# Norm weight carried by the weights, sums of x kept in memory, and slots bound to operands in the two gate passes, with the mLSTM core's first tiles on those slots

## The chip, the core and the metric

The kernel runs on one core of one Trainium2 chip. A core has five engines, each with its own in-order queue: TensorE (PE, matmuls; its weight loads are shown as PEld), VectorE (DVE), ScalarE (ACT), GpSimd (POOL) and SyncE (SP), which here issues the transfers (DMAs). Instructions wait for each other through semaphores, so an instruction that waits holds up everything behind it in its own queue. The metric is device microseconds of one execution; lower is better.

## The reference

Two layers on 2048 + 256 tokens of width 1024: windowed attention, then a bidirectional mLSTM, each behind a norm and with a gated output. The change lies in the mLSTM layer and in what leads to it. What is computed there, cut to the essentials:

```
x2 = x + attention(rms_norm(x, g0))
xn = rms_norm(x2, g1)                      # x2 * rstd * g1
q, k, v, gates, o, z = split(xn @ w_in)    # 512, 512, 1024, 16, 1024, 1024 columns
h  = mlstm(q, k, v, gates)                 # forward and backward, chunks with carried state C, n, m
h  = rms_norm(h per head) * sigmoid(o) * silu(z)
y  = rms_norm(x2 + h @ w_out, final_g)
```

## The kernel before

**Tiles.** The tokens are 18 tiles of 128 (2048 tokens are 16 tiles, the 256 others two). Everything is float32; each operand of a product is split into a high part in the format that TensorE multiplies (ACT makes it: `hi`) and the rest (DVE makes it: `lo = x - hi`), and a product is three matmuls, hi*hi, hi*lo and lo*hi.

**Passes.** A projection of 1024 columns goes through `winograd_pass` (L335). It works on nine pairs of tiles. `quarters` (L200) loads the weight in sixteen pieces of 128 x 512 and splits them into weight slots. The first pair is multiplied in the plain way (L320 to L322); halfway through it `combinations` (L212) makes four combined operands t1 to t4 of the weight in place of loaded pieces, and the other eight pairs are multiplied by Winograd's form of Strassen's scheme, seven products instead of eight (L271 to L273). For it `winograd_x` (L237) makes four sums of the input pieces (L249, L250, L256, L261 on DVE) and splits seven operands for each pair. Five such passes run: z of the attention, its output, q and k of the mLSTM (`mlstm_qkv`, L639), and two for the gates o and z (`mlstm_gates_states`, L813; pass 0 and pass 1, together "the oz passes"), which also carry the backward state of the mLSTM, tile by tile. The narrower v and gate projections (L666 to L682) run in the plain way between the q,k pass and the oz passes.

**Norm.** `attn_out` (L603) adds the residual, takes the norm and transposes; the transposed tile leaves PSUM through a DVE multiplication by g1 (L633) and is stored as `xn2T`, the input of the q,k, v and oz projections.

**Gates.** `gate_sums` (L685) turns the gate columns of all tiles into running maxima and decay factors. It is one serial chain of small operations over PE, DVE and ACT: sums (L710, L716), a transpose (L723), a maximum (L725), a row of running maxima of 36 + 32 tiny DVE operations (L741, L744), exponentials (L748, L755), two scans (L767) and their exponentials (L768, L775). It is written ahead of the oz passes and its pool is called `gt`.

**Core.** `mlstm_core` (L864) runs over the tiles: weights of a tile (`E`, `El`, `Eh`, split v), four heads of numerators (L926, L928), the state update (L806), the gating (L944), and then the output projection of the tile before (`back`, L376 to L378 with the weight w_mo from L992), with the final norm.

**Order.** The code is recorded through a tile framework which then orders the instructions of each engine by a simulated timeline, so instructions of the next stage can stand among those of the stage before. Three things limit this: each queue runs in order; a tile whose memory was used before waits for the last reader of what lay there (the pools of different stages share addresses); SP issues transfers in eight lanes, and a transfer waits for the one eight before it. Weight slots are taken from one list, `self.free`, whichever is free first (L132). The sixteen slots of pool `wp` stay; eight more (`y0` to `y7` in pool `wy`, L1008) lie where the core's right-hand pool `b3y` (L869) comes to lie afterwards. The oz passes hold their gate tiles `e` and `s` in pool `b2`, which is opened before `b2s`, the pool of the backward state (L816, L817).

Of the kernel before, what the change touches and what calls it, by code (L numbers as in the profile page):

```python
# [48 lines left out]
KX, WL = 0, 0  # L49
# [12 lines left out]
class Trunk:  # L62
    def __init__(self, nc, tc, ctx, a):
# [120 lines left out]
    def part(self, raw, g=None):  # L184

        nc = self.nc
        hi, lo = self.slot()
# [12 lines left out]
    def quarters(self, src, c0, g=None):  # L200

        W = {k: [None] * 4 for k in ("b12", *WOPS)}
        for row in range(2):
            gk = lambda i: None if g is None else g[:, row * 4 + i:row * 4 + i + 1]
            for i in range(4):
                for col in range(2):
                    op = f"b{row + 1}{col + 1}"
                    W[op][i] = self.part(self.quarter(src, c0, row, col, i), gk(i))
# [3 lines left out]
    def combinations(self, src, c0, W, g=None):  # L212
# [9 lines left out]
        for i in range(4):  # L222
# [10 lines left out]
            for op, raw in (("t2", t2), ("t3", b12), ("t1", b11), ("t4", b21)):  # L233
                W[op][i] = self.part(raw)
                self.at[op, i] = self.taken.pop()

    def winograd_x(self, s0, s1, X):  # L237

# [4 lines left out]

        a11 = load(s0, 0)
# [5 lines left out]
        nc.vector.tensor_sub(x2, x1, a11)  # L250
        X["s2"] = self.split(x2)
# [4 lines left out]
        nc.vector.tensor_sub(a21, a11, a21)  # L256
        X["s3"] = self.split(a21)
# [3 lines left out]
        nc.vector.tensor_sub(a12, a12, x2)  # L261
# [73 lines left out]
    def winograd_pass(self, xT, src, c0, g, use, done=None, following=None, first=None):  # L335
# [267 lines left out]
    def attn_out(self, first):  # L603
        nc, tc, a = self.nc, self.tc, self.a
        with ExitStack() as st:
# [18 lines left out]
            def norm(t, x):  # L624
                rs = p.tile([128, 1], F32, tag="rs", name="rs", bufs=2)
                self.rms(p, x, rs[:])
                for b in range(2):
# [5 lines left out]
                    nc.vector.tensor_mul(xo[:], tp[:], self.g[:, 1, b * 4:(b + 1) * 4].unsqueeze(2).to_broadcast([128, 4, 128]))  # L633
# [155 lines left out]
    def weighted_k(self, p, t, d, raw=()):  # L789
# [4 lines left out]
        hi = p.tile([128, MH, DQK], F32R, tag="kh", name="kh", bufs=1)  # L794
        nc.gpsimd.tensor_mul(k, k, self.w[:, d, t, :].unsqueeze(2).to_broadcast([128, MH, DQK]))
# [17 lines left out]
    def mlstm_gates_states(self):  # L813
        nc, tc, a = self.nc, self.tc, self.a
        with ExitStack() as st:
            pe = st.enter_context(tc.tile_pool(name="b2", bufs=2, reuse_waits="tile"))  # L816
            p = st.enter_context(tc.tile_pool(name="b2s", bufs=1, reuse_waits="tile"))  # L817
# [22 lines left out]
            for b in range(2):  # L840
# [3 lines left out]
                def use(t, h, o, u, b=b):  # L844
# [5 lines left out]
                    nc.scalar.activation(e, o, AF.Sigmoid)  # L850
                    if h == 0:
                        (nc.vector if u is None else nc.gpsimd).tensor_mul(e, e, o)
                    if t not in part:
# [6 lines left out]
                X = self.winograd_pass(self.xn2T, a["w_oz"], b * 1024, None, use, lambda n, pair: back_state(NT - 1 - b * len(PAIRS) - n),  # L860
                                       self.xn2T[:2] if b == 0 else None, X)


    def mlstm_core(self, y):  # L864
        nc, tc, a = self.nc, self.tc, self.a
        with ExitStack() as st:
            pool = lambda n, **k: st.enter_context(tc.tile_pool(name=n, bufs=2, reuse_waits="tile", **k))
            TRP, TRT = self.sps, "s"
            py, pm, pv, p, pe = pool("b3y", side="right"), pool("b3m"), pool("b3v"), pool("b3"), self.early  # L869
            ps = pool("b3ps", space=PSUM)  # L870
            cm = py.tile([128, 2, 128], F32, tag="cm", name="cm", bufs=1)
# [7 lines left out]
            def weights(t):  # L879
# [8 lines left out]
                v = self.parts(pv, self.v[t], "v", 2)  # L888
                qs = (py if t % 2 else pv).tile([128, 2, MH, 128], F32, tag="qs", name="qs", bufs=1)
# [221 lines left out]
```

## Time and profile before

| | |
|---|---|
| time, median of 3 runs | 2311.11 us (2309.26 to 2311.87) |
| profiled execution | 2308.62 us |
| span of its profile | 2306.6 us |
| PE busy | 2216.3 us, 96% |
| DVE busy | 1561.6 us, 68% |
| ACT busy | 1094.6 us, 47% |
| POOL busy | 468.2 us, 20% |
| DMA | 326.41 MB |
| TensorE clock granted, mean | 0.987 |

The stages follow each other as: attention to about 700 us, its z gate and its output to 1094 us, q and k from there to 1300 us, v to 1490 us, the two oz passes to 1894.5 us, the core to the end. A row of the timeline reads: start, duration, engine, line, operation, out<-in with the tiles' names, shapes, count, and in brackets the idle time of the engine before it and what released it.

### The profile page before, as it was taken

The numbers are of one execution on the slowest core, as the hardware profiler recorded it, in microseconds if no ns is written. First come the engines' busy times: TensorE is split into PE (matmuls) and PEld (weight loads), VectorE is DVE, ScalarE is ACT, GpSimd is POOL, SyncE is SP. The second block draws the span as 40 slices with busy tenths as digits, with TensorE's granted clock in tenths as the row PEclk, the third lists the DMA queues.
The fourth block names the chain that finished last, engine by engine and source line by source line (L and its number), as shares of the span: only waits on it lengthen the run. The fifth ranks groups of instructions, "written<-read, shape, count | busy, mean of one in ns | idle before, by whom it ended". The sixth has DMA issues, their size and how long they took to land.

```text
span 2306.6 us, 32951 instructions
## 1 busy us (share of the span) xinstructions
PE 2216.3 (96%) x11102; PEld 1763.1 (76%) x11102; DVE 1561.6 (68%) x3403; ACT 1094.6 (47%) x2503; POOL 468.2 (20%) x392
## 2 busy tenths in 40 slices
PE   8999999999899999999899999999999987999998
PEld 7767676767567888788788899978877876888887
DVE  7565656565877779778656422487888676777784
ACT  6454545454764335445434311346454355455453
POOL 3211121211001222232000000022232234333320
PEclk9999999999999999999999999999999997999999
DMA  7111111111226447667534622344465456665642
GB/s 266 48 39 49 38 49 39 49 38 40 92 65 196 152 159 239 219 214 237 172 123 145 222 92 92 122 157 154 164 215 174 146 188 222 216 197 196 209 157 69
DMA packets 170281, 326.41 MB, mean 142 GB/s; under 512 B 18784, under 2 KB 21632, under 8 KB 170112
## 3 DMA queue, kind: packets, MB, share of 16 engines
q1 hardware_dynamic: 169968, 324.30, 42.2%
q8 instruction: 88, 1.44, 0.3%
q14 instruction: 81, 0.66, 0.1%
q10 hardware_dynamic: 144, 0.01, 0.0%
HBM read 235.34 MB, written 88.89 MB: 141 GB/s over the span
## 4 chain that ended last, share of the span: by engine, by line
PE 75%; DVE 10%; DMA 5%; ACT 4%; issue 3%; POOL 2%; SPq 0%; DVEq 0%; POOLq 0%; ACTq 0%
PE pj L376 9%; PE pj L378 9%; PE pj L377 9%; PE pj L271 4%; PE pj L272 4%; PE pj L273 4%; PE ptp L527 3%; PE o L539 3%; PE d L271 3%; PE d L272 3%; PE c L273 3%; PE d L273 3%; PE c L272 3%; PE c L271 3%; DMA qs<-rows 2%
## 5 line engine op out<-in xcount | busy, mean ns | idle before, releaser
L376 PE MATMUL pj<-whi,xhi 128*128 128x512 f32 (+2 forms) x1152 | 433.8, 378 | 8.6 <-ACT whi L167 5.6
L122 ACT CAST xhi<-rawx 128x512 fp32r<-128x512 f32 x372 | 228.3, 618 | 439.9 <-PE pj L377 106.4
L378 PE MATMUL pj<-whi,xlo 128*128 128x512 f32 (+2 forms) x1152 | 422.8, 372 | 5.2 <-DVE xlo L123 4.4
L377 PE MATMUL pj<-wlo,xhi 128*128 128x512 f32 (+2 forms) x1152 | 426.4, 370 | 0.0
L123 DVE TENSOR_TENSOR xlo<-rawx,xhi 128x512 fp32r<-128x512 f32 x338 | 246.0, 732 | 81.3 <-ACT xhi L122 73.5
L376 PEld LDWEIGHTS pj<-whi,xhi 128*128 128x128 f32 x1152 | 218.1, 189 | 50.8 <-issue 8.8
L378 PEld LDWEIGHTS pj<-whi,xlo 128*128 128x128 f32 x1152 | 217.7, 189 | 49.5 <-DVE xlo L123 8.6
L377 PEld LDWEIGHTS pj<-wlo,xhi 128*128 128x128 f32 x1152 | 217.9, 189 | 37.0 <-issue 2.4
L514 ACT ACTIVATE Sm<-Sm,nm 128x384 f32<-128x384 f32 (+1 forms) x288 | 167.1, 582 | 94.3 <-DVE nm L508 87.9
L271 PE MATMUL pj<-whi,xhi 128*128 128x512 f32 x480 | 193.9, 404 | 7.2 <-DVE u L286 2.7
L272 PE MATMUL pj<-wlo,xhi 128*128 128x512 f32 x480 | 192.3, 401 | 2.9 <-DVE wlo L190 2.9
L273 PE MATMUL pj<-whi,xlo 128*128 128x512 f32 x480 | 191.6, 400 | 0.0
L503 DVE CUSTOM_DVE_ANT_0 Sm<-s,mask 128x384 f32<-128x384 f32 (+1 forms) x272 | 136.0, 530 | 72.8 <-PE s L501 69.9
L527 PE MATMUL ptp<-ident,Sm 128*128 128x128 f32 x800 | 135.5, 280 | 10.0 <-DVE PT L530 6.6
L527 PEld LDWEIGHTS ptp<-ident,Sm 128*128 128x128 f32 x800 | 94.6, 141 | 54.6 <-ACT Sm L514 19.2
L271 PE MATMUL d<-whi,xhi 128*128 128x512 f32 x320 | 128.0, 400 | 0.0
L273 PE MATMUL c<-whi,xlo 128*128 128x512 f32 x320 | 127.3, 398 | 0.0
L272 PE MATMUL c<-wlo,xhi 128*128 128x512 f32 x320 | 127.3, 398 | 0.0
L271 PE MATMUL c<-whi,xhi 128*128 128x512 f32 x320 | 127.2, 397 | 0.0
L272 PE MATMUL d<-wlo,xhi 128*128 128x512 f32 x320 | 126.7, 396 | 0.0
L273 PE MATMUL d<-whi,xlo 128*128 128x512 f32 x320 | 126.6, 396 | 0.0
L500 PE MATMUL s<-KH,Q 128*128 128x384 f32 (+1 forms) x288 | 106.1, 380 | 10.3 <-DVE mx L503 4.6
(243 smaller groups left out, 4670.8 us busy)
## 6 DMA issues: line engine op xcount, KB each, us to landing
rawx<-xn2T SPq DMA_DIRECT2D x144, 256.0 KB, 3.1
x<-x SPq DMA_DIRECT2D x108, 256.0 KB, 3.9
rawx<-xT SPq DMA_DIRECT2D x72, 256.0 KB, 2.9
raww<-w_oz SPq DMA_DIRECT2D x64, 256.0 KB, 5.1
raww<-w_qkvg SPq DMA_DIRECT2D x40, 256.0 KB, 3.8
v<-v SPq DMA_DIRECT2D x18, 516.0 KB, 3.7
rawx<-v SPq DMA_DIRECT2D x36, 258.0 KB, 2.8
rawx<-x SPq DMA_DIRECT2D x36, 256.0 KB, 3.0
```

The lines of the kernel that those rows point to most:

```text
L122: nc.scalar.copy(hi[:], src)
L123: (eng or nc.vector).tensor_sub(lo[:], src, hi[:].bitcast(F32))
L271: nc.tensor.matmul(o, xh, wh, start=i == 0 and not more, stop=False, skip_group_check=more)
L272: nc.tensor.matmul(o, xh, wl, start=False, stop=False, skip_group_check=more)
L273: nc.tensor.matmul(o, xl, wh, start=False, stop=i == 3, skip_group_check=more)
L376: nc.tensor.matmul(o[:, :n], xh, wh, start=kt == 0, stop=False)
L377: nc.tensor.matmul(o[:, :n], xh, wl, start=False, stop=False)
L378: nc.tensor.matmul(o[:, :n], xl, wh, start=False, stop=kt == KT - 1)
L500: nc.tensor.matmul(S[:, :nk, :], q, KH[:, g, win, :], start=True, stop=False)
L503: nc.vector.tensor_tensor_reduce(Sm[:, :nk], S[:, :nk], mask[:, t % 3, win, :], 1.0, MASKED, ALU.add, ALU.max, mx[:, c:c + 1])
L514: nc.scalar.activation(Sg[c][:, :nk], Sg[c][:, :nk], AF.Exp, bias=nm[:, c:c + 1], scale=HD ** -0.5, accum_out=rs[:, c:c + 1])
L527: nc.tensor.transpose(tp[:, c, :], Ss[g][c][:, j, :], self.ident[:])
```

## The change

1. **Norm weight.** `attn_out` copies the transposed tile with ACT, without g1. The q,k pass, the v projection and the oz passes multiply g1 into their weights: the split of a piece becomes an ACT copy with a scale and a DVE operation with a scale, and `combinations` gets two ACT multiplications for each of its four steps.
2. **Sums of x.** The q,k pass stores the four sums of each of its eight Winograd pairs (32 stores of 256 KB). The oz passes load seven pieces per pair instead of four and make no sums.
3. **Slots.** In the oz passes an operand may have slots of its own: y0 to y3 hold only b11, y4 to y7 hold only b21 (pass 0) or t2 (pass 1). The v stage gets a list of slots without five of the free ones.
4. **Core.** The right-hand pool `b3y` holds what the core's first tiles need (v, qs, El, Eh of tile 0), other tiles alternate between pools; `cm` moves to the pool that is opened early; w_mo is loaded after six steps of the core's first tile, its transfers and splits ordered behind the last sigmoid of the oz passes; the weighted k of the forward state is made by four ACT copies with a scale and four DVE operations per tile instead of one POOL, one ACT and one DVE operation.
5. **Pools.** `b2s` is opened before `b2`.

```diff
-    def slot(self):
-        pool, tag = self.free.popleft()
+    def slot(self, op=None):
+        own = self.own.get(op)
+        others = [x for tags in self.own.values() for x in tags]
+        pick = next(x for x in self.free if (x in own if own else x not in others))
+        self.free.remove(pick)
+        pool, tag = pick
...
-    def winograd_x(self, s0, s1, X):
+    def winograd_x(self, s0, s1, X, sums=None):
+        if sums:
+            at = {"a11": (s0, 0), "a12": (s0, 1), "a22": (s1, 1), **{f"s{i + 1}": (s, 0) for i, s in enumerate(sums)}}
+            for op in XOPS:
+                X[op] = self.split(load(*at[op]))
+                yield
+            return
+        def keep(i, x):
+            if sums is not None:
+                d = self.dp.tile([128, 512], F32, tag=f"xs{len(self.xs)}_{i}", name="xsum")
+                made[i] = d
+                nc.sync.dma_start(d[:], x)
...
-                    nc.vector.tensor_mul(xo[:], tp[:], self.g[:, 1, b * 4:(b + 1) * 4].unsqueeze(2).to_broadcast([128, 4, 128]))
+                    nc.scalar.copy(xo[:], tp[:])
...
-            self.winograd_pass(self.xn2T, a["w_qkvg"], 0, None, use, first=first)
-            w = self.load_w(a["w_qkvg"][:, 1024:], [[512], [272, 256]])
+            self.winograd_pass(self.xn2T, a["w_qkvg"], 0, self.g[:, 1], use, first=first, sums=True)
+            kept = self.first + [[x for x in self.free if x not in self.first][-1]]
+            self.free = deque(x for x in self.free if x not in kept)
+            w = self.load_w(a["w_qkvg"][:, 1024:], [[512], [272, 256]], self.g[:, 1])
             self.release()
+            self.free.extendleft(reversed(kept))
...
+        if d == 0:
+            for h in range(MH):
+                wk = self.w[:, d, t, h:h + 1]
+                nc.scalar.activation(hi[:, h], k[:, h], AF.Copy, scale=wk)
+                nc.vector.scalar_tensor_tensor(lo[:, h], k[:, h], wk, hi[:, h].bitcast(F32), ALU.mult, ALU.subtract)
+            return hi, lo
...
+            p = st.enter_context(tc.tile_pool(name="b2s", bufs=1, reuse_waits="tile"))
             pe = st.enter_context(tc.tile_pool(name="b2", bufs=2, reuse_waits="tile"))
-            p = st.enter_context(tc.tile_pool(name="b2s", bufs=1, reuse_waits="tile"))
...
-                    nc.scalar.activation(e, o, AF.Sigmoid)
+                    self.gated = nc.scalar.activation(e, o, AF.Sigmoid)
...
-                X = self.winograd_pass(self.xn2T, a["w_oz"], b * 1024, None, use, lambda n, pair: back_state(NT - 1 - b * len(PAIRS) - n),
+                self.own = {"b11": self.first, "t2" if b else "b21": self.second}
+                X = self.winograd_pass(self.xn2T, a["w_oz"], b * 1024, self.g[:, 1], use, lambda n, pair: back_state(NT - 1 - b * len(PAIRS) - n),
...
-            py, pm, pv, p, pe = pool("b3y", side="right"), pool("b3m"), pool("b3v"), pool("b3"), self.early
+            py, pv, pm, p, pe = pool("b3y", side="right"), pool("b3v"), pool("b3m"), pool("b3"), self.early
...
-                v = self.parts(pv, self.v[t], "v", 2)
-                qs = (py if t % 2 else pv).tile([128, 2, MH, 128], F32, tag="qs", name="qs", bufs=1)
+                v = self.parts(pv if t % 2 else py, self.v[t], "v", 1)
+                qs = (pv if t % 2 else py).tile([128, 2, MH, 128], F32, tag="qs", name="qs", bufs=1)
...
-                El = p.tile([128, 2, MH, 128], F32R, tag="El", name="El", bufs=2)
+                El = (p if t % 2 else py).tile([128, 2, MH, 128], F32R, tag="El", name="El", bufs=1)
...
-            if not WL:
-                w += self.load_w(a["w_mo"], [[512]] * 2, self.g[:, 2], PH3, PL3)
...
-                    if t == 0 and i == WL and WL:
-                        w += self.load_w(a["w_mo"], [[512]] * 2, self.g[:, 2], PH3, PL3)
+                    if t == 0 and i == WL:
+                        with tc.issue_after(self.gated.ins):
+                            w += self.load_w(a["w_mo"], [[512]] * 2, self.g[:, 2], PH3, PL3)
```

**PE at the start of oz pass 0.** In the names, `um` is the maximum of `gate_sums`, `rw` its row of running maxima, `pl` and `pr` its PSUM tiles, `cu` the backward state's; `pj`, `c` and `d` are the PSUM tiles of the passes. Before, two excerpts where products of the chain stand:

```order
L271 MATMUL pj<-whi,xhi 128x512
L272 MATMUL pj<-wlo,xhi 128x512
L273 MATMUL pj<-whi,xlo 128x512
L272 MATMUL pj<-wlo,xhi 128x512
L728 MATMUL pr<-ident,um 1x72 x2
L273 MATMUL pj<-whi,xlo 128x512
L271 MATMUL pj<-whi,xhi 128x512
```

```order
L271 MATMUL pj<-whi,xhi 128x512
L753 MATMUL pl_14942<-rw,ones 128x144
L272 MATMUL pj<-wlo,xhi 128x512
L273 MATMUL pj<-whi,xlo 128x512
L750 MATMUL pl<-spr,ones 128x144
L271 MATMUL pj<-whi,xhi 128x512
```

After, the end of the plain pair (L347 to L349 are its matmuls now, L298 to L300 those of a Winograd pair):

```order
L349 MATMUL c<-whi,xlo 128x512
L936 MATMUL s<-qT,kT 128x128 x4
L759 MATMUL pr<-ident,um 1x72 x2
L784 MATMUL pl_15014<-rw,ones 128x144
L781 MATMUL pl<-spr,ones 128x144
L791 MATMUL pm<-ones,rw 72x1 x2
L804 MATMUL pM<-ident,MT 128x72 x2
L843 MATMUL cu<-vh,kh 128x258
L843 MATMUL cu<-v,kh 128x258
L843 MATMUL cu<-vh,kl 128x258
```

Nine matmuls into `cu` stand there, and behind them the first `L298` into `pj`. The chain's products stood one by one among the Winograd pairs (L728 in pair 1, L753 further on); now all of them stand in one row between the plain pair and the first Winograd pair.

**ACT at the same place.** `e<-pj` and `e<-c` are the sigmoids that empty the plain pair's PSUM tiles. Before:

```order
L850 ACT_TABLE_LOAD
L850 ACTIVATE e<-pj 128x512
L189 CAST whi<-raww 128x512 x2
L850 ACTIVATE e<-pj 128x512
L189 CAST whi<-raww 128x512 x3
L122 CAST xhi<-rawx 128x512
L850 ACTIVATE e<-c 128x512
```

After:

```order
L779 ACT_TABLE_LOAD
L779 ACTIVATE spr<-spr 1x144
L786 ACTIVATE scr<-scr 128x144
L799 ACTIVATE sT<-MT,msc 72x128
L833 CAST kh<-rawk 128x512
L799 ACTIVATE sT<-MT,msc 72x128
L806 ACTIVATE scr<-scr 128x144
L845 COPY C<-cu 128x258
L887 ACT_TABLE_LOAD
L887 ACTIVATE e<-pj 128x512 x2
L887 ACTIVATE e<-c 128x512
```

The first sigmoid stood ahead of the whole chain and now stands behind its last exponential (L806) and the first `C` of the backward state. The memory of `e` and `s` now lies on that of `gt`; before, that of `b2s` did.

**ACT where the oz passes end and the core starts.** `e<-s` is the last sigmoid, `whi` a high part of w_mo, `E` the core's weights, `hh` the first head's output. Before:

```order
L906 ACT_TABLE_LOAD
L906 ACTIVATE E<-E,scr 128x128 x8
L850 ACT_TABLE_LOAD
L850 ACTIVATE e<-s 128x512
L908 CAST Eh<-E 128x512 x2
L906 ACT_TABLE_LOAD
L906 ACTIVATE E<-E,scr 128x128 x8
L908 CAST Eh<-E 128x512 x2
L906 ACTIVATE E<-E,scr 128x128
L785 CAST vh<-rawx 128x516 x4
```

After:

```order
L947 CAST Eh<-E 128x512 x2
L887 ACTIVATE e<-s 128x512
L173 ACTIVATE whi<-raww,g 128x512 x6
L945 ACT_TABLE_LOAD
L945 ACTIVATE E<-E,scr 128x128 x3
L173 ACTIVATE whi<-raww,g 128x512
L945 ACTIVATE E<-E,scr 128x128
L845 COPY C<-cu 128x258
L945 ACTIVATE E<-E,scr 128x128 x4
L973 ACTIVATE hh<-num,r 128x256
```

Before, the sixteen exponentials of tiles 0 and 1 and the first two splits of v stand around and behind the last sigmoid. Now tile 0's stand back in pass 0, and behind the last sigmoid come splits of w_mo (six, then one, the others among the heads; before, the last of them stood just ahead of this place) and eight exponentials, which are of tile 2; those of tile 1 come after the first heads.

More of the change, by code (lines that the diff above doesn't have):

```diff
@@ L83, in __init__ @@
         self.wp = ctx.enter_context(tc.tile_pool(name="w", bufs=1))
+        self.own = {}
         self.free = deque((self.wp, f"w{i}") for i in range(16))
+        self.xs = []
         self.sp = ctx.enter_context(tc.tile_pool(name="stage", bufs=1))
@@ L182, in release, with part @@
         self.taken = []
-    def part(self, raw, g=None):
+    def part(self, raw, g=None, op=None):
         nc = self.nc
-        hi, lo = self.slot()
+        hi, lo = self.slot(op)
         if g is None:
@@ L207, in quarters @@
                     op = f"b{row + 1}{col + 1}"
-                    W[op][i] = self.part(self.quarter(src, c0, row, col, i), gk(i))
+                    W[op][i] = self.part(self.quarter(src, c0, row, col, i), gk(i), op)
                     self.at[op, i] = self.taken.pop()
@@ L250, in winograd_x @@
         nc.vector.tensor_sub(x2, x1, a11)
+        keep(1, x2)
+        keep(0, x1)
         X["s2"] = self.split(x2)
@@ L264, in winograd_x @@
         X["s4"] = self.split(a12)
+        if sums is not None:
+            self.xs.append([made[i] for i in range(4)])
         yield
@@ L333, in plain, with winograd_pass @@
             side()
-    def winograd_pass(self, xT, src, c0, g, use, done=None, following=None, first=None):
+    def winograd_pass(self, xT, src, c0, g, use, done=None, following=None, first=None, sums=False):
         self.at = {}
@@ L352, in winograd_pass @@
             if n + 1 < len(PAIRS):
-                gen = self.winograd_x(xT[pair[0] + 2], xT[pair[1] + 2], nxt)
+                gen = self.winograd_x(xT[pair[0] + 2], xT[pair[1] + 2], nxt, (self.xs[n] if n < len(self.xs) else ()) if sums else None)
             else:
@@ L868, in mlstm_core @@
             TRP, TRT = self.sps, "s"
-            py, pm, pv, p, pe = pool("b3y", side="right"), pool("b3m"), pool("b3v"), pool("b3"), self.early
+            py, pv, pm, p, pe = pool("b3y", side="right"), pool("b3v"), pool("b3m"), pool("b3"), self.early
             ps = pool("b3ps", space=PSUM)
-            cm = py.tile([128, 2, 128], F32, tag="cm", name="cm", bufs=1)
-            nc.sync.dma_start(cm[:], a["causal"])
+            cm = self.cm
             w = []
+            ring = self.rings["raww"]
+            self.rings["rawk"] = deque(ring.pop() for _ in range(2))
+            self.own = {}
             fg = pm.tile([128, D], F32, tag="fg", name="fg", bufs=1)
-            nc.sync.dma_start(fg[:], a["final_g"].to_broadcast([128, D]))
             state = {0: None}
@@ L952, in update @@
                     return
-                kw = self.weighted_k(py, t, 0, () if t < KX else ("raww",))
+                kw = self.weighted_k(pv, t, 0, ("rawk",))
                 yield
@@ L969, in back @@
                     yield
-                x = [p.tile([128, 512], F32, tag="x", name="x", bufs=3)[:] for b in range(2)]
+                x = [pm.tile([128, 512], F32, tag="x", name="x", bufs=3)[:] for b in range(2)]
                 for b in range(2):
@@ L1008, in run @@
         with tc.tile_pool(name="wy", bufs=1, side="right") as wy:
-            self.free.extend((wy, f"y{i}") for i in range(8))
+            ys = [(wy, f"y{i}") for i in range(8)]
+            self.free.extend(ys)
+            self.first, self.second = ys[:4], ys[4:]
             self.attn_core()
@@ L1026, in run @@
                 self.early = ctx.enter_context(tc.tile_pool(name="b3e", bufs=2, reuse_waits="tile"))
+                self.cm = self.early.tile([128, 2, 128], F32, tag="cm", name="cm", bufs=1)
+                nc.sync.dma_start(self.cm[:], a["causal"])
                 self.mlstm_gates_states()
```

10 lines of the change are left out of this document (7 added, 3 removed).

## The prediction

> **What bounds the kernel now.** Busy time first: PE is busy 96% of the span, so the time is PE's work plus the places where PE waits. A cut in another engine's work is worth something only at those places. The table by stages finds them (columns: busy time and instruction count of PE, PE loads, DVE, ACT and POOL, then granted clock, DMA share, GB/s).
>
> ```profile
> 880.00:1065.00 185.00, 183.87 (x859) 149.90 (x858) 146.12 (x244) 92.26 (x184) 49.20 (x39) 1.00 0.68 223
> 1065.00:1300.00 235.00, 226.91 (x1075) 186.29 (x1074) 152.81 (x256) 105.59 (x194) 8.31 (x8) 0.98 0.53 175
> 1300.00:1490.00 190.00, 190.00 (x1199) 172.08 (x1198) 45.96 (x94) 35.82 (x59) 1.70 (x16) 1.00 0.31 106
> 1490.00:1680.00 190.00, 186.42 (x865) 151.54 (x864) 157.32 (x311) 100.08 (x173) 46.86 (x31) 1.00 0.50 167
> 1680.00:1890.00 210.00, 203.12 (x905) 165.16 (x904) 165.68 (x259) 94.25 (x164) 56.35 (x35) 0.98 0.51 169
> 1890.00:1940.00 50.00, 24.79 (x122) 20.68 (x121) 33.35 (x62) 31.48 (x77) 29.48 (x23) 0.76 0.74 260
> 1940.00:2260.00 320.00, 314.80 (x1740) 271.22 (x1739) 244.53 (x601) 166.08 (x464) 105.41 (x91) 0.99 0.57 191
> ```
>
> PE waits 8.1 us where q,k starts, nothing in the v stage, 3.6 us in oz pass 0, 6.9 us around the start of oz pass 1, 25.2 us where the core starts, and 5.2 us in the whole rest of the core. All that the change can take away is in these 49 us, and half of it is at the core's start; the order of the attention core is not touched.
>
> **Part by part: oz pass 0, where I expect the loss.** First the timeline of PE (start, duration) behind the plain pair, and of DVE and ACT beside it:
>
> ```profile
> 1516.27 0.40 PE L322 MATMUL c<-whi,xlo 128*128 128x512 f32 x1
> ...
> 1523.65 0.50 PE L271 MATMUL pj<-whi,xhi 128*128 128x512 f32 x1 [0.91 <-ACT whi L189]
> ...
> 1535.23 0.47 PE L271 MATMUL pj<-whi,xhi 128*128 128x512 f32 x1 [2.20 <-DVE u L286]
> ```
>
> ```profile
> 1516.08 0.67 DVE L218 TENSOR_TENSOR raww<-raww 128x512 f32<-128x512 f32 x1
> 1516.68 1.27 DVE L190 TENSOR_TENSOR wlo<-raww,whi 128x512 fp32r<-128x512 f32 x2
> ...
> 1519.09 0.41 DVE L724 COPY uT<-pu 72x256 f32<-72x256 f32 x1
> ...
> 1540.88 0.23 DVE L744 TENSOR_TENSOR rw<-rw,be 1x4 f32<-1x4 f32 x2
> 1541.06 0.23 DVE L741 TENSOR_TENSOR rw<-umr,rw 1x4 f32<-1x4 f32 x2
> ...
> 1550.77 0.30 DVE L747 TENSOR_TENSOR spr<-rw 1x144 f32<-1x144 f32 x1
> ```
>
> ```profile
> 1508.31 1.28 ACT L850 ACT_TABLE_LOAD   x1
> 1509.60 0.60 ACT L850 ACTIVATE e<-pj 128x512 f32<-128x512 f32 x1
> ...
> 1555.52 0.32 ACT L755 ACTIVATE scr<-scr 128x144 f32<-128x144 f32 x1 [2.24 <-DVE scr L754]
> ```
>
> PE goes from the plain pair (end 1516.7) straight into the Winograd products, since the first sigmoid has emptied a PSUM tile at 1509.6. The gate chain runs beside it for 32 us (`uT` at 1519.1, `spr` at 1550.8) and nobody waits. In the order after, PE has the whole chain between the plain pair and the first Winograd pair, and ACT has its first sigmoid behind the chain, because `e` lies on the chain's memory. So what was beside PE's work is now PE's wait. Its length:
> - The transpose into `pu` stands 23 matmuls ahead of the plain pair's end. At 0.23 us apart (12 matmuls take 2.8 us), and with the plain pair ending as before, `uT` can be made from 1512 on. I take 1514; where it was before, 1519.1, is the late end.
> - From `uT` to `spr` DVE has 16 operations 512 wide in the order after (0.60 us apart, rows at 1516.08 and 1516.68: 9.7 us), the 68 steps of `rw` (pairs 0.18 us apart, rows at 1540.88 and 1541.06: 6.2 us) and small ones (0.4): 16.3 us. `spr` is done at 1530.3, up to 6 us later where DVE waits for ACT or a transfer.
> - From there the chain goes on to the backward state and the sigmoid, with these rows:
>
> ```profile
> L795 POOL TENSOR_TENSOR rawk<-rawk,scr 128x512 f32<-128x512 f32 x16 | 19.1, 1193 | 87.2 <-DMA rawk<-k 44.5 <-DVE u L286 17.3 <-DVE rawx L261 10.8
> L796 ACT CAST kh<-rawk 128x512 fp32r<-128x512 f32 x16 | 9.9, 618 | 2.5 <-PE cu L806 2.5
> L797 DVE TENSOR_TENSOR kl<-rawk,kh 128x512 fp32r<-128x512 f32 x16 | 12.3, 770 | 0.0
> L808 ACT COPY C<-cu 128x258 f32<-128x258 f32 x16 | 5.7, 370 | 1.3 <-PE cu L806 1.2
> L852 DVE TENSOR_TENSOR e<-e,pj 128x512 f32<-128x512 f32 x20 | 13.6, 678 | 0.8 <-ACT e L850 0.8
> ```
>
> Table load 1.28 and exponential 0.32, products and copies 0.5, exponential of w 0.32, k by w 1.19, kh 0.62, kl 0.77, products of the state 0.5, C 0.37, table load 1.28, sigmoid 0.60, DVE 0.68: 8.4 us. PE starts the Winograd pairs at 1538.7 to 1544.7, 22 to 28 us behind the plain pair. Of this it works some 3.7 us (my estimate: four scores 1.0, half of the eight in the row at 1902.65 below; nine into `cu` at 0.28, the row at 1927.35, 2.5; the chain's own 0.2), so it idles 18 to 24 us where it idled 3.6. One more wait of about 1 us follows, since the copy `u` of pair 1 stands behind tile 0's exponentials on ACT.
> - Clock: after the idle at the core's start PE ran slow,
>
> ```profile
> 1918.10 0.42 PE L926 MATMUL num<-v,Eh 128*128 128x258 f32 x1
> ...
> 1927.35 0.28 PE L926 MATMUL num<-v,Eh 128*128 128x258 f32 x1
> ```
>
> 0.42 us for what takes 0.28 later, and the stage's granted clock is 0.76. I count 1.6 us for one such stretch here (estimate: a third of some 5 us). Sum: 21 + 1 - 3.6 + 1.6 = **+20**, from +14 (`uT` at 1512, every operand ready, no cold stretch) to +27 (6 us of waits on DVE).
>
> The Trainium skill ("ScalarE: Activation LUTs", "What ACT_TABLE_LOAD costs") puts a switch at 2.66 us, the load and a drain of 1380 ns. Here the sigmoid starts 1.29 us after the load's start, so the row shows no drain; by the page the chain's two loads would add an estimated 2.8 us, by the trace nothing.
>
> **The core's start, where the gain is.** PE around the last product of the oz passes, T0 = 1894.5:
>
> ```profile
> 1894.14 0.39 PE L273 MATMUL d<-whi,xlo 128*128 128x512 f32 x1
> 1902.65 2.05 PE L897 MATMUL s<-qT,kT 128*128 128x128 f32 x8 [8.12 <-DVE E L907]
> 1916.45 0.58 PE L926 MATMUL num<-vh,Eh 128*128 128x258 f32 x1 [11.75 <-ACT vh L785]
> ...
> 1941.70 0.99 PE L376 MATMUL pj<-whi,xhi 128*128 128x512 f32 x1
> ```
>
> The first head starts 22 us after T0, the first projection at T0 + 47.2. After the change tile 0's weights are ready, so heads 0 and 1 start at about T0. But PSUM holds two heads, and the third needs the first `hh` on ACT, which stands behind eight exponentials of tile 2. What such exponentials, POOL's addition ahead of them and the transfer of a tile's `E` took (in the list of transfers the last number is the median to landing), and the mean of a split of w_mo (ns, last before the second bar):
>
> ```profile
> 1907.13 2.44 ACT L906 ACTIVATE E<-E,scr 128x128 f32<-128x128 f32 x8 [1.02 <-DVE E L904]
> ```
>
> ```profile
> 1914.20 2.48 POOL L904 TENSOR_TENSOR E<-E,cm 128x512 f32<-128x512 f32 x2
> ```
>
> ```profile
> E<-rows SPq DMA_DIRECT2D x18, 512.0 KB, 5.1
> ```
>
> ```profile
> L171 DVE SCALAR_TENSOR_TENSOR wlo<-raww,g,whi 128x512 fp32r<-128x512 f32 x40 | 37.1, 961 | 4.3 <-ACT whi L167 4.2
> ```
>
> DVE makes the last `s`, two splits of v and two `El`, five operations of 0.60 to 0.67, by T0 + 3.4; only then is tile 0's `E` free for tile 2. Transfer 5.1, POOL 2.48, exponentials 2.44, first `hh` 0.5: T0 + 14. From there DVE has, ahead of the first projection, nine splits of w_mo (done before T0 until now; 0.74 alone, L193's row below, 0.96 in the mean: 7 to 9 us), eight other wide operations (5) and about 30 small ones (8): 20 to 22 us, with waits for ACT and POOL 22 to 25. The first projection comes at T0 + 36 to 39 and not 47.2, but about two heads (2 us of PE) are still undone then. Gain 47.2 - 37.5 - 2 = **-8**, from -13 (no waits in those 20 us, POOL at once) to -2 (six more of waits).
>
> **Start of oz pass 1.** PE idles 6.9 us there:
>
> ```profile
> 1725.33 0.80 PE L272 MATMUL pj<-wlo,xhi 128*128 128x512 f32 x1 [2.85 <-DVE wlo L190]
> ```
>
> ```profile
> 1690.00:1744.00 54.00, 47.12 (x197) 37.15 (x196) 48.19 (x78) 23.55 (x43) 18.41 (x7) 0.92 0.63 206
> ```
>
> ```profile
> L193 DVE SCALAR_TENSOR_TENSOR wlo<-raww,g,whi 128x512 fp32r<-128x512 f32 x16 | 11.2, 740 | 0.0
> L228 ACT ACTIVATE raww<-raww,g 128x512 f32<-128x512 f32 x4 | 2.9, 724 | 4.6 <-DVE raww L226 4.6
> ```
>
> DVE is busy 48 of 54 us and ends most waits. The change takes eight sums (8 x 0.60 = 4.8 us) from DVE there and adds scales (28 operations, 0.74 and not 0.67: 2.0 us); ACT gets eight multiplications at 0.72 and 16 scales (0.72 and not 0.62: 7.4 us), with 30 idle. **-4**, from -7 (all idle gone) to +3 (`combinations` now goes from DVE to ACT and back for each step). The Trainium skill ("SBUF — State Buffer") says that a DVE operation with two SBUF inputs and a GpSimd operation lock each other out; the sums are of this kind, and the term would go to -7 with it. No row here separates that from DVE's own load.
>
> **The rest.** The start of q,k loses eight DVE multiplications of L633 (4.8 us) and gets 2.0 of scales; ACT gets eight copies (0.6) and the same 7.4, 12 us, in a stretch where it idles 19 of 41, and the wait there is ended by ACT, not DVE:
>
> ```profile
> 1112.32 1.12 PE L658 MATMUL tr<-ident,q 128*128 128x128 f32 x4 [8.09 <-ACT q L650]
> ```
>
> ```profile
> 1071.00:1112.00 41.00, 33.23 (x156) 27.02 (x154) 40.01 (x66) 22.28 (x43) 7.47 (x7) 0.94 0.74 246
> ```
>
> So **0**, from -5 to +5. Elsewhere the moved multiplications and the 48 dropped sums lie under a full PE (first row of the stages): 0. The v stage is full too, with ACT and DVE idle three quarters: 0. The 32 stores and 48 added loads (21 MB) lie under DMA shares of 0.5: 0, and +3 if loads come late. The core later: ACT and DVE get some 2 us per tile, POOL loses 1.2, PE idles 5.2 in all: **-1**, from -4 to +4.
>
> **Sum:** 20 - 8 - 4 + 0 - 1 = +7 on 2308.62 = 2315.6. This execution lies 2.5 us below the median of 2311.11, so on that scale the forecast is **2318 us**.
>
> **Rivals.** (a) *Faster: PE runs through into the core.* If tile 2's `E` comes early, or ACT's wait for it is short, the first `hh` comes at T0 + 4 rather than 14, and the gain at the core's start rises from 8 to 18 or more, up to the whole 22 us idle and 2 us of cold clock. With +18 in pass 0 and -6 in pass 1 this gives 2311 + 18 - 24 - 6 = 2299. It decides from a first `hh` before about T0 + 2: the core has to give back 20 + 4.6 - 4 - 1, some 20 us, 12 more than I forecast. For it: the heads' operands are there. Against: ACT's order, in which `hh` cannot pass the exponentials. Chance 0.10. (b) *Same:* chain short (+15), core -12, pass 1 -5: 2309; all between 2306.5 and 2315.7. Chance 0.25. (c) *The core still waits:* the splits of w_mo, in turns on ACT and DVE behind the late `hh`, eat the whole gain; then +20 + 3 + 0 + 0 = 2334. The change would not do there what it says. For it: fourteen splits moved behind T0. Chance 0.12. My forecast has 0.53, with 2316 to 2326.
>
> **Numbers.** 0.2% (4.6 us) is about what a measurement of this kernel can tell from no change. Faster 0.10, same 0.25, slower 0.65 (0.53 + 0.12). The range goes from 2304, a little into (a), to 2333, most of (c).
>
> **What would show it.** In the profile after: PE idle of 18 to 24 us between the plain pair and the first Winograd pair of pass 0, with the first sigmoid at its end and behind the last exponential of the gates; heads 0 and 1 within 2 us of T0, then a wait that ends at the first `hh` near T0 + 14; the first projection near T0 + 37; less than 4 us of idle at the start of pass 1; PE as before in the v stage. Wrong would be: Winograd products before the chain's end, or a third head before T0 + 8.

## The result, and the profile after

| | before | after |
|---|---|---|
| median | 2311.49 us (2308.96 to 2315.42, 6 runs) | 2324.73 us (2319.94 to 2326.18, 6 runs) |
| profiled execution | 2308.62 us | 2325.41 us |
| PE busy, of the span | 2216.3 us, 96% | 2223.3 us, 96% |
| DVE, ACT, POOL busy | 1561.6, 1094.6, 468.2 us | 1503.4, 1138.8, 431.9 us |
| DMA | 326.41 MB | 347.41 MB |

The changed kernel is slower: ratio 1.0053, 95% interval 1.0041 to 1.0065. The forecast was 2318 us, 2304 to 2333. VectorE does 58 us less and GpSimd 36 us less, and the kernel loses 13 us; so the work was not where the time was. The table by stages of the changed kernel, cut where its own stages lie (columns as in the prediction):

```profile
1065.00:1300.00 235.00, 229.68 (x1086) 188.23 (x1085) 153.67 (x254) 121.70 (x220) 9.36 (x9) 0.99 0.65 218
1300.00:1490.00 190.00, 190.00 (x1191) 171.78 (x1190) 42.18 (x88) 33.35 (x54) 1.69 (x16) 1.00 0.31 106
1490.00:1520.00 30.00, 29.48 (x156) 24.43 (x154) 22.60 (x46) 20.72 (x34) 0.00 (x0) 1.00 0.74 248
1520.00:1560.00 40.00, 19.68 (x81) 15.61 (x80) 28.82 (x112) 25.25 (x45) 4.64 (x4) 0.70 0.47 154
1700.00:1760.00 60.00, 58.10 (x259) 46.30 (x258) 57.58 (x87) 36.26 (x65) 13.04 (x8) 1.00 0.80 264
1905.00:1960.00 55.00, 34.99 (x157) 28.44 (x155) 43.12 (x85) 36.87 (x92) 19.52 (x14) 0.78 0.68 234
1960.00:2280.00 320.00, 310.20 (x1708) 265.34 (x1706) 245.17 (x630) 171.17 (x496) 93.10 (x86) 0.99 0.57 191
```

Three places differ from before: 20.3 us of idle at 1520 to 1560 at a clock of 0.70, which is new; 1.9 us at the start of pass 1 where there were 6.9; and the core's start, where PE still idles 20 of 55 us. PE's timeline gives the limits of the stages. Of the changed kernel (end of the plain pair, first Winograd matmul, pass 1, last oz product, first projection, last projection):

```profile
1518.86 0.40 PE L349 MATMUL c<-whi,xlo 128*128 128x512 f32 x1
...
1521.68 0.41 PE L759 MATMUL pr<-ident,um 72*1 72x72 f32 x4 [1.53 <-DVE um L756]
1537.00 0.81 PE L784 MATMUL pl<-rw,ones 1*128 1x144 f32 x2 [14.91 <-DVE rw L772]
...
1545.95 0.79 PE L298 MATMUL pj<-whi,xhi 128*128 128x512 f32 x1 [1.62 <-DVE e L889]
...
1710.50 0.39 PE L347 MATMUL pj<-whi,xhi 128*128 128x512 f32 x1
...
1907.22 0.40 PE L300 MATMUL d<-whi,xlo 128*128 128x512 f32 x1
...
1947.10 0.79 PE L403 MATMUL pj<-whi,xhi 128*128 128x512 f32 x1 [0.68 <-ACT xhi L124]
...
2316.20 0.40 PE L405 MATMUL pj<-whi,xlo 128*128 128x512 f32 x1
```

Of the kernel before, the two limits that the prediction did not show (start of pass 1, last projection):

```profile
1688.15 0.39 PE L320 MATMUL pj<-whi,xhi 128*128 128x512 f32 x1
...
2298.44 0.40 PE L378 MATMUL pj<-whi,xlo 128*128 128x512 f32 x1
```

| from one profile to the other | before | after | difference |
|---|---|---|---|
| to the end of the plain pair of pass 0 | 1516.7 | 1519.3 | +2.6 |
| from there to the start of pass 1 | 171.5 | 191.2 | **+19.7** |
| pass 1, to the last oz product (T0) | 206.4 | 197.1 | **-9.3** |
| from T0 to the last projection | 404.3 | 409.0 | **+4.7** |

Of the first line 1.0 us is there at 715 us already, before anything that the change touches. Each kernel has one profile, and runs of one kernel lie up to 14 us apart (30 runs of the kernel before: 2302.54 to 2316.17 us), so a difference of a few us in one stage can be that execution's own.

### The profile page after: what moved, and what is told of

It reads as the page before. It is cut to its first block, busy times and chain, and to the rows that moved or that the text cites. A ratio compares the mean times of both kernels' runs of the same rounds, so it can differ in the third digit from the quotient of the medians.

```text
span 2323.6 us, 33181 instructions
## 1 busy us (share of the span) xinstructions
PE 2223.3 (96%) x11102; PEld 1765.5 (76%) x11102; DVE 1503.4 (65%) x3351; ACT 1138.8 (49%) x2608; POOL 431.9 (19%) x376
## 2 busy tenths in 40 slices
DMA packets 181804, 347.41 MB, mean 150 GB/s; under 512 B 20065, under 2 KB 22913, under 8 KB 181633
## 5 line engine op out<-in xcount | busy, mean ns | idle before, releaser
L298 PE MATMUL pj<-whi,xhi 128*128 128x512 f32 x480 | 192.7, 401 | 3.9 <-DVE e L889 2.8
L299 PE MATMUL pj<-wlo,xhi 128*128 128x512 f32 x480 | 191.2, 398 | 0.0
L300 PE MATMUL pj<-whi,xlo 128*128 128x512 f32 x480 | 191.0, 399 | 0.0
L298 PE MATMUL d<-whi,xhi 128*128 128x512 f32 x320 | 127.9, 400 | 1.2 <-DVE x L645 1.2
L298 PE MATMUL c<-whi,xhi 128*128 128x512 f32 x320 | 127.1, 397 | 0.0
L300 PE MATMUL c<-whi,xlo 128*128 128x512 f32 x320 | 127.0, 397 | 0.0
L300 PE MATMUL d<-whi,xlo 128*128 128x512 f32 x320 | 126.3, 395 | 0.0
```

Of the source, the lines that this page charges most:

```text
L298: nc.tensor.matmul(o, xh, wh, start=i == 0 and not more, stop=False, skip_group_check=more)
L299: nc.tensor.matmul(o, xh, wl, start=False, stop=False, skip_group_check=more)
L300: nc.tensor.matmul(o, xl, wh, start=False, stop=i == 3, skip_group_check=more)
```

## The experiments

Twelve kernels ran. "Oz 0", "oz 1" and "core" are the last three rows of that table, from the profile of each. Each of the groups e1 to e4, e5 to e8, e9 to e11 and e12 has its own runs of the kernel before (medians 2311.16, 2310.28, 2311.56 and 2310.66 us), so medians are compared within a group and ratios across groups.

| run | median us | ratio to before, 95% | oz 0 | oz 1 | core |
|---|---|---|---|---|---|
| before | 2310 to 2312 | 1 | 171.5 | 206.4 | 404.3 |
| after | 2324.73 | 1.0053 (1.0041 to 1.0065) | 191.2 | 197.1 | 409.0 |
| e1, pools back | 2305.03 | 0.9973 (0.9961 to 0.9984) | 177.1 | 194.5 | 407.5 |
| e2, weighted k back | 2319.25 | 1.0033 (1.0021 to 1.0045) | 191.3 | 198.9 | 402.2 |
| e3, w_mo not held | 2324.02 | 1.0056 (1.0044 to 1.0068) | 192.6 | 197.3 | 405.7 |
| e4, before with the new pool order | 2319.86 | 1.0037 (1.0025 to 1.0049) | 189.2 | 200.1 | 405.6 |
| e5, pools and weighted k back | 2301.28 | 0.9964 (0.9951 to 0.9977) | 176.4 | 194.9 | 405.0 |
| e6, e5 and w_mo not held | 2304.70 | 0.9977 (0.9965 to 0.9990) | 175.9 | 198.1 | 406.8 |
| e7, e5 without stored sums | 2306.21 | 0.9979 (0.9970 to 0.9988) | 171.2 | 201.8 | 409.4 |
| e8, e5 with the norm weight in xn2T | 2305.26 | 0.9981 (0.9969 to 0.9994) | 179.9 | 196.9 | 404.6 |
| e9, e5 with w_mo partly on GpSimd | 2309.99 | 0.9994 (0.9983 to 1.0004) | 176.1 | 195.2 | 412.3 |
| e10, before with the new weighted k | 2313.06 | 1.0009 (0.9998 to 1.0020) | 173.2 | 207.2 | 409.4 |
| e11, e1 with k in eight pieces | 2337.84 | 1.0119 (1.0104 to 1.0134) | 176.3 | 194.7 | 441.4 |
| e12, parts 1 and 2 on before | 2304.35 | 0.9962 (0.9947 to 0.9976) | 171.1 | 198.4 | 409.2 |

**The pool order (e1, e4).** The edit of e1, on the changed kernel; e4 makes the opposite edit on the kernel before:

```diff
-            p = st.enter_context(tc.tile_pool(name="b2s", bufs=1, reuse_waits="tile"))
             pe = st.enter_context(tc.tile_pool(name="b2", bufs=2, reuse_waits="tile"))
+            p = st.enter_context(tc.tile_pool(name="b2s", bufs=1, reuse_waits="tile"))
```

> The changed kernel with the two pools of the oz passes opened in the old order again (gate tiles' pool before the backward state's), nothing else. Theory A: the pool order alone puts the gate tiles on the memory of the gate sums, and that makes TensorE wait out the chain; then the 21 us of idle at the start of pass 0 shrink to under 5 and the kernel gets 17 to 22 us faster than the changed one, 0.987 to 0.997 of before. Rival B: the wait comes from the later q,k and x-sum transfers or from the core's early tiles; then the chain stays between the plain pair and the first Winograd pair and the ratio stays near 1.005.

> The kernel before with only the two pools of the oz passes opened in the new order. Theory A: this alone makes the wait of pass 0; ratio 1.006 to 1.010 with some 20 us of TensorE idle between the plain pair and the first Winograd pair. Rival B: without the rest of the change the chain is early enough to be hidden; ratio within 0.002 of 1.

With the pools in the old order the median is 19.7 us below the changed kernel's (18.5 by the two ratios) and 0.27% below that of before. e4, with this one edit, has the wait of pass 0 in the kernel before. PE's timeline of e4 behind the plain pair:

```profile
1524.18 0.64 PE L728 MATMUL pr<-ident,um 72*1 72x72 f32 x4 [5.27 <-DVE um L725]
1533.30 0.81 PE L753 MATMUL pl<-rw,ones 1*128 1x144 f32 x2 [8.48 <-DVE rw L741]
...
1542.24 0.79 PE L271 MATMUL pj<-whi,xhi 128*128 128x512 f32 x1 [1.61 <-DVE e L852]
```

And of e1 at the same place, its three longest waits before 1545:

```profile
1524.46 0.50 PE L298 MATMUL d<-whi,xhi 128*128 128x512 f32 x1 [0.76 <-ACT e L887]
1527.71 0.50 PE L298 MATMUL pj<-whi,xhi 128*128 128x512 f32 x1 [1.36 <-ACT u L310]
...
1537.73 0.77 PE L298 MATMUL pj<-whi,xhi 128*128 128x512 f32 x1 [3.75 <-DVE e L889]
```

Rivals B of both fall: the pool order alone makes the wait, in either kernel. That it does so through the shared memory is read from the pools' layout; no run separates the two. e4 loses 8.7 us over all (ratio 1.0037, under theory A's 1.006) where its pass 0 loses 17.7, in part since its pass 1 got 6.3 us shorter with no edit there; why that is so is not shown.

e1 does not take back all of pass 0: 177.1 us are 5.6 more than before. Its longest wait, 3.75 us for `e`, ends with a DVE operation at 1536.92. That one stands behind steps of the gate chain and follows ACT's sigmoid at 1534.00, ahead of which ACT had waited for a piece of the weight:

```profile
1532.35 0.73 ACT L198 ACTIVATE whi<-raww,g 128x512 fp32r<-128x512 f32 x1 [3.64 <-DMA raww<-w_oz]
```

e5 has the same wait (3.81 us, with 3.71 of ACT for the weight); e7, without the stores and loads of the sums, has not, and its pass 0 takes 171.2 us. This fits the prediction's "+3 if loads come late", but does not show it: the order is another in e7, and e12 has the sums and no such loss (171.1).

**The weighted k (e2, e10, e11).** e2 takes part 4's new form of the weighted k out of the changed kernel, e10 puts it into the kernel before:

```diff
-        if d == 0:
-            for h in range(MH):
-                wk = self.w[:, d, t, h:h + 1]
-                nc.scalar.activation(hi[:, h], k[:, h], AF.Copy, scale=wk)
-                nc.vector.scalar_tensor_tensor(lo[:, h], k[:, h], wk, hi[:, h].bitcast(F32), ALU.mult, ALU.subtract)
-            return hi, lo
         nc.gpsimd.tensor_mul(k, k, self.w[:, d, t, :].unsqueeze(2).to_broadcast([128, MH, DQK]))
```

e11 is e1 with each head's piece made in two halves (`for c in (slice(0, 64), slice(64, 128))`).

> The changed kernel with the weighted k of the forward state made as before (one GpSimd multiplication, one ScalarE cast, one VectorE subtraction). Theory A: the four VectorE operations per tile cost the core's steady part a little, since TensorE waits there for VectorE's split of the transposed tile; then the 3.7 us lost between tile 1 and the end come back, ratio 1.002 to 1.004. Rival B: the core's loss is all in its first two tiles; then the ratio stays 1.005 and the waits for the split stay as in the changed kernel.

> The kernel before with only the weighted k of the forward state changed (four ScalarE copies and four VectorE operations per tile). Theory A: the 64 small VectorE operations take 41 us and not the 19 of the sixteen large ones, and TensorE waits for VectorE's splits in the core; ratio 1.001 to 1.003, the stretch from the last oz product to the end 3 to 7 us longer than 404.3. Rival B: they cost only beside the w_mo splits of the changed kernel; ratio within 0.001 of 1.

> The run with only the pools put back, with the weighted k in eight pieces per tile and not four. Theory A: a small VectorE operation there takes 0.67 us in the mean where two of them ran in 0.61, since each waits for what GpSimd has running; eight pieces then take VectorE to 60 us or more, and the core gets 4 to 8 us longer, 2309 to 2313 us. Rival B: the cost goes by the elements; eight pieces take about 45 us and the time stays within 2 us of 2305.

e2 gives 5.5 us back in the median (4.6 by the ratios, whose intervals just overlap), and in its profile the core is 6.8 us shorter (409.0 to 402.2). By its ratio theory A of e2 holds, by the place it does not: 5.0 of the 6.8 us lie in the first 66 us behind T0 (idle, and what is lost where the granted clock is 0.50, called half clock; counted as further below) and 1.3 behind them. In the list of costly groups DVE's part of it is, in the changed kernel (64 pieces of the forward, 16 whole ones of the backward state), in e2 (32 whole ones) and in e11:

```profile
L830 DVE SCALAR_TENSOR_TENSOR kl<-rawk,scr,kh 128x128 fp32r<-128x128 f32 x64 | 41.0, 671 | 0.2 <-ACT kh L829 0.2
L834 DVE TENSOR_TENSOR kl<-rawk,kh 128x512 fp32r<-128x512 f32 x16 | 10.9, 680 | 0.5 <-issue 0.3 <-ACT kh L833 0.2
```

```profile
L828 DVE TENSOR_TENSOR kl<-rawk,kh 128x512 fp32r<-128x512 f32 x32 | 30.5, 953 | 0.5 <-issue 0.3 <-ACT kh L827 0.2
```

```profile
L831 DVE SCALAR_TENSOR_TENSOR kl<-rawk,scr,kh 128x64 fp32r<-128x64 f32 x128 | 44.8, 410 | 0.0
```

51.9 us against 30.5. Why a quarter of the elements takes as long as all of them, DVE and POOL of the changed kernel show in one tile:

```profile
2098.69 1.33 DVE L830 SCALAR_TENSOR_TENSOR kl<-rawk,scr,kh 128x128 fp32r<-128x128 f32 x1
2099.94 0.14 DVE L970 SCALAR_TENSOR_TENSOR r<-num,scr 128x2 f32<-128x2 f32 x1
2100.01 1.58 DVE L830 SCALAR_TENSOR_TENSOR kl<-rawk,scr,kh 128x128 fp32r<-128x128 f32 x2
2101.51 0.14 DVE L971 TENSOR_TENSOR r<-r,num 128x2 f32<-128x2 f32 x1
2101.58 0.34 DVE L830 SCALAR_TENSOR_TENSOR kl<-rawk,scr,kh 128x128 fp32r<-128x128 f32 x1
```

```profile
2098.57 2.61 POOL L943 TENSOR_TENSOR E<-E,cm 128x512 f32<-128x512 f32 x2 [3.65 <-DMA E<-rows]
```

POOL runs two additions of 1.3 us from 2098.57 to 2101.18. The first two pieces take 1.33 and 1.32 us and end 0.15 us behind them, at 2100.0 and 2101.3; the last two take 0.34 each. It is so throughout: of the 64 pieces 23 take 0.65 to 1.47 us, and each of them ends 0.15 us behind a POOL operation. In e2 eleven of the whole operations in the core take 1.08 to 1.77 us, and each ends 0.55 us behind one addition. So a whole operation waits for one addition, and of four pieces often two wait. This is the rule that the prediction set against the row at the start of pass 1 (the Trainium skill, "SBUF — State Buffer", "Who interferes with whom": a DVE operation with two SBUF inputs contends with a GpSimd operation that reads SBUF); here the trace agrees, 1.33 us against 0.34. At the start of pass 1 it was not at work on the sums: before the change all eight of them between 1690 and 1744 took 0.67 to 0.69 us. Neither theory of e11 holds, though: DVE's time rises little against e1 (39.2 to 44.8 us, as rival B had it), but the core gets 34 us longer. Behind its first 66 us PE idles 32.1 us where e1 has 8.9, and loses 12.9 to half clock where e1 has 1.7. PE waits for the split of the transposed tile, 26.0 us in ten waits behind 1950 (e1: 4.4 in eight). In one of them, here on DVE and PE, five pieces stand ahead of that split in DVE's queue:

```profile
2058.26 3.12 DVE L831 SCALAR_TENSOR_TENSOR kl<-rawk,scr,kh 128x64 fp32r<-128x64 f32 x5
2061.30 0.68 DVE L817 TENSOR_TENSOR v<-rawx,vh 128x516 fp32r<-128x516 f32 x1
...
2061.98 0.68 DVE L817 TENSOR_TENSOR v<-rawx,vh 128x516 fp32r<-128x516 f32 x1
2062.58 0.68 DVE L125 TENSOR_TENSOR xlo<-tr,xhi 128x512 fp32r<-128x512 f32 x1
```

```profile
2063.32 0.50 PE L405 MATMUL pj<-whi,xlo 128*128 128x512 f32 x1 [3.04 <-DVE xlo L125]
```

So in e11 the price of the slow small operations was set by what stands behind them, and the order is made anew for each kernel. Twice as many small operations stand on ACT too (32.6 us for 20.6), and no run separates the two. e10 (ratio 1.0009, interval 0.9998 to 1.0020) is inconclusive: its core took 5.0 us more in the one profile, but so did that of e12 (4.9), where nothing in the core was edited. That the new weighted k costs time in the core therefore rests on e2 alone.

**The splits of w_mo (e3, e6, e9).** e3 is the changed kernel, e6 is e5 with this edit:

```diff
-                        with tc.issue_after(self.gated.ins):
+                        if True:
```

e9 is e5 with `PH3, PL3 = (), (3, 6)`, by which GpSimd does the multiplication and subtraction of four of the sixteen splits.

> The changed kernel with the loads and splits of w_mo not held behind the last sigmoid, nothing else. Theory A: the splits of w_mo behind the last sigmoid eat the gain at the core's start (the first two tiles took 29 us and not 22 between their transposes); without the hold they go back under the oz pass, and the stretch from the last oz product to the end shrinks by 8 to 14 us, ratio 0.999 to 1.002. Rival B: they only fill idle time of VectorE, and the wait for tile 2's row of weights sets the start; then less than 3 us come back, ratio over 1.004.

> As the run before, with the loads and splits of w_mo not held behind the last sigmoid. Theory A: with the first heads no longer behind tile 2's exponentials, the splits of w_mo are what is left of work at the core's start; 3 to 6 us come back, ratio 0.992 to 0.994. Rival B: as in the run without the hold alone, the stretch from the last oz product to the end gets some 3 us shorter and the oz pass as much longer, ratio as in the run before, within 0.001.

> As the run with pools and weighted k undone, and four of the sixteen splits of w_mo done by GpSimd (multiplication and subtraction) in place of VectorE. Theory A: VectorE, busy in 7 to 10 of every 10 us of the first 40 us behind the last oz product, is the bound there, and the lead of tile 0 (transposed 14 us earlier than before the change) is lost at tile 1 because the splits of w_mo stand on VectorE; with some 3 us less on it the stretch to the end gets 2 to 5 us shorter than 405.0, ratio 0.993 to 0.9955. Rival B: GpSimd is as much in the way (its additions for tiles 2 and 3 come later, and operations of the two hold each other up); the stretch stays at 404 to 408, ratio 0.996 to 0.998.

None helps. Without the hold the core gets 3.3 us shorter in e3, far from the 8 to 14 of theory A, and 1.8 longer in e6, where pass 1 gets 3.1 longer; on GpSimd the splits cost 0.3% (ratio 0.9994 for 0.9964), and the core takes 7.3 us more. So theory A, that the splits of w_mo on DVE eat the gain, fails in all three. Rival B is met by its ratio in e3 (1.0056); in e6 and e9 it points the right way, but the core comes out longer than it said (406.8 and 412.3).

**What can be had together (e5, e7, e8, e12).** e5 makes e1's and e2's edits. e7 is e5 with `sums=True` and the last argument `True` of the oz passes taken out; e8 is e5 with the DVE multiplication by g1 in `attn_out` and plain weights in its three places; e12 is the kernel before with only those two parts put in.

> The changed kernel with both undone that cost time: the pool order of the oz passes and the weighted k. Theory A: the two are separate places (start of pass 0, core), so their effects add: 2305.0 less the 5.5 us that the weighted k gave alone, about 2299.5, ratio 0.994 to 0.9965. Rival B: the weighted k cost only because the core's first tiles were late; then nothing is left of it here, ratio 0.997 as with the pools alone.

> As the run with pools and weighted k undone, and the sums of x made again in the oz passes (no stores, four loads per pair). Theory A: the stored sums relieve VectorE at the start of pass 1, which lasted 194.6 us with them and 206.4 before; without them it takes 3 to 8 us more, ratio 0.996 to 0.998. Rival B: the gain of pass 1 comes from the later order of work there (it shrank to 200.1 us also when only the pools were exchanged in the kernel before), and the stored sums give under 2 us.

> As the run with pools and weighted k undone, and the norm weight again multiplied into xn2T by VectorE in attn_out, with plain weights. Theory A: the norm weight in the weights is neutral, as forecast for the start of q,k (VectorE gives, ScalarE takes): ratio within 0.001 of that run. Rival B: the extra step from VectorE to ScalarE and back in each combination delays the combined weights of three passes; then this run is 2 to 5 us faster than that run.

> The kernel before with parts 1 and 2 of the change alone (norm weight in the weights, sums of x stored); its slots, its core and its pool order stay as before. Theory A: the gain of the repaired kernels sits in the oz passes, where the start of pass 1 lost 11 us to idle and half clock before and 1 to 2 us after, and the core's early start is worth nothing, since its scattered waits leave TensorE idle or at half clock as much as the one long wait did; then this kernel reaches 2300 to 2304, ratio 0.995 to 0.9975, like the run with pools and weighted k undone. Rival B: the early slots are what relieves pass 1 or the core; then it stays at 2307 or more, ratio 0.998 to 1.000.

e5 is 0.36% faster than before; its interval holds the ratios of both its theories, so it does not say whether the two effects add. e12 reaches the same (0.38%) with the core, the slots and the pools of before; its passes lie at 171.1 and 198.4 us, and by its ratio theory A of e12 holds. So what is good in the change are parts 1 and 2, and the work of parts 3 and 4 on the core's start brings nothing that these runs can see. Which of the two parts gives it is open: taking either out of e5 costs 4 to 5 us in the median, but the intervals of e5, e7 and e8 overlap. e7 loses 6.9 us in pass 1, as its theory A had it, gains 5.2 in pass 0, and its core, with no edit there, takes 4.4 more. e8 is slower than e5 and not faster, so its rival B falls; its ratio is 0.0017 above e5's where theory A had 0.001, which the intervals do not tell apart.

## Why the prediction was right, and where its terms were off

**Pass 0, +20: measured +19.7.** The mechanism is shown by e1 and e4: the wait goes and comes with the pool order. Of the 19.7 us e1 takes back 14.1, and e4 makes 17.7 in the kernel before; the 5.6 us that e1 keeps are waits of its own, for which the sum had nothing. Step by step: `uT` came at 1519.6 and not 1514, just behind the late end of 1519.1; from there to the end of `spr` 17.5 us and not 16.3; from there to the first Winograd matmul 8.8 and not 8.4; idle 20.3, in the 18 to 24. ACT shows the end of the chain:

```profile
1542.89 0.38 ACT L845 COPY C<-cu 128x258 f32<-128x258 f32 x1 [0.81 <-PE cu L843]
1543.28 1.28 ACT L887 ACT_TABLE_LOAD   x1
1544.58 1.08 ACT L887 ACTIVATE e<-pj 128x512 f32<-128x512 f32 x2
```

The load starts as the copy ends, and the sigmoid again starts 1.30 us after the load's start, with no drain to be seen. Two small terms were off: the clock, forecast at 1.6 us, cost 4.0, and the further wait of 1 us did not come (the whole pass idles 20.3 us). For the clock I sum PE's busy time in windows of 2 us times what the granted clock there lacks to 1, here and below; this is the loss called half clock.

**Pass 1, -4: measured -9.3.** The direction was right; the term left out the clock. Before, PE lost 6.9 us to idle and 4.3 to half clock in this pass, with four waits of 1.1 to 2.9 us between 1718 and 1740; after, 1.9 and none. Both passes as PE's windows give them, before and after:

```profile
1688.00:1894.00 206.00, 199.12 (x885) 161.78 (x884) 162.37 (x252) 92.89 (x161) 58.00 (x36) 0.98 0.49 164
```

```profile
1710.00:1907.00 197.00, 195.10 (x884) 158.71 (x883) 133.29 (x212) 92.01 (x163) 45.99 (x34) 1.00 0.61 202
```

DVE's busy time falls by 29 us there. The gain needs no wait in pass 0 (e4, which has the wait alone, got 6.3 us): e1, which has none, takes 194.5 us.

**The core, -8 and -1: measured +4.7.** Here the sum failed. Its steps came as forecast: heads 0 and 1 start at once, the first `hh` comes behind tile 2's exponentials at T0 + 15.6 (forecast 14), and the first projection begins at T0 + 39.5 (36 to 39).

```profile
1908.76 0.40 PE L965 MATMUL num<-vh,Eh 128*128 128x258 f32 x2
...
1912.97 0.58 PE L965 MATMUL num<-vh,El 128*128 128x258 f32 x1 [2.63 <-DVE El L948]
...
1922.18 0.58 PE L843 MATMUL cu<-vh,kh 128*128 128x258 f32 x1 [5.40 <-ACT C L845]
1924.24 0.58 PE L965 MATMUL num<-vh,Eh 128*128 128x258 f32 x1 [1.04 <-DVE hh L974]
...
1933.64 0.39 PE L843 MATMUL cu<-vh,kh 128*128 128x258 f32 x1 [4.00 <-ACT C L845]
```

The step that failed is "47.2 - 37.5 - 2": an earlier first projection is not an earlier end. Before, PE waited almost in one piece, 8.1 and 11.8 us with 2 us of work between them. After, it waits in eleven pieces of 0.4 to 5.4 us over 60 us, with work at half clock between them. The first 66 us behind T0, before, after and in e1:

```profile
1894.00:1960.00 66.00, 40.79 (x205) 34.58 (x204) 44.25 (x90) 38.28 (x99) 34.60 (x27) 0.79 0.69 241
```

```profile
1907.00:1973.00 66.00, 43.47 (x192) 35.41 (x191) 52.16 (x101) 41.05 (x107) 24.37 (x18) 0.79 0.65 223
```

```profile
1887.00:1953.00 66.00, 47.28 (x216) 38.44 (x214) 55.47 (x114) 44.49 (x116) 24.16 (x19) 0.77 0.70 231
```

Idle falls by 2.7 us (by 6.5 in e1), the mean clock does not rise, and the work now done at half clock costs 10.4 us (9.7 in e1) where it cost 5.7. That is +2.0, and 2.1 us more idle follow up to tile 17, where my term had -1; e2 says that the weighted k has its part in this. So 4.1 of the 4.7 us are placed. Rival (c) named this outcome for the core, with a cause that e3, e6 and e9 did not bear out.

How much of the +4.7 is the change's is open. e12, whose core starts as before (first projection at T0 + 49.0), takes 409.2 us too; its first 66 us:

```profile
1885.00:1951.00 66.00, 39.69 (x190) 34.14 (x191) 43.16 (x83) 38.53 (x98) 33.92 (x27) 0.74 0.69 232
```

Idle and half clock together are 27.9 to 33.5 us there in the four profiles with the old start (before, e4, e10, e12) and 24.9 to 32.9 in the ten with the new one. What the runs do show is that the 9 us forecast for the core are in none of them: with the new start the core takes 402.2 us at the least, with the old one 404.3.

**The rest.** The start of q,k was forecast at 0 and came 1.1 us later, as late as the stages ahead of it; the v stage stayed full; of the 21 MB more of DMA nothing is seen in the changed kernel, and e1's wait in pass 0 leaves it open. From profile to profile the span rose by 17.0 us (the four differences, 17.7, and 0.7 less behind the last projection) where the forecast had 7. The missing 10.0 are +2.6 ahead of the end of the plain pair (1.0 of them there before the change's first operation), -0.3 in pass 0, -5.3 in pass 1, +13.7 in the core and -0.7 behind it. So the direction and the pool order's price were foreseen. The core's term had the wrong sign, and it was luck that pass 1 gained 5.3 us more than forecast and hid part of that. The median rose by less, 13.2, since the profiled execution of before lay 2.9 us below its median and that of after 0.7 above.

## What to carry to other kernels

Before a pool is opened in another order, look whose memory its first tiles get: a tile on the memory of a long serial chain can make that chain the critical path, however little work it has (one swapped line cost 19.7 us in the changed kernel and 8.7 in the kernel before). Breaking one long wait of PE into many gained nothing here that the runs can tell: count the time at half clock with the idle. And cutting DVE's operations into pieces did not divide what they lost to POOL's: in the core the pieces of fifteen tiles took 39.9 us, e2's whole operations 18.9.

## What was not expected of the hardware

PE's granted clock stayed at 0.50 for about 20 us on end in e1 (1901.5 to 1921.8), while PE was busy for 11.25 of 20.50 us, 55%. The windows of e1 give it (stretch, its length, busy time of PE, weight loads, DVE, ACT and POOL, the clock):

```profile
1900.60:1921.10 20.50, 11.25 (x41) 8.38 (x40) 17.79 (x31) 17.86 (x49) 9.05 (x8) 0.52 0.85 285
```

No single wait there was longer than 3.5 us. The busy stretches between the waits were 0.8 to 3.7 us long, and the clock came back only in the one that began at 1917.14, some 4.7 us behind its start. And DVE operations of 0.34 us took up to 1.47 us beside POOL's operations of 1.3 us, each slow one ending 0.15 us behind one of these.
